# Keeping the S5, GLU and first-norm instructions of a hybrid backbone block in their emitted order on each engine

## Chip, cores and metric

The kernel runs on one core of one Trainium2 chip. The metric is the time of one execution in device microseconds (us). The kernel before takes 1634.49 us, the median of three runs (1630.75, 1634.49 and 1637.27 us).

## What is computed

The block has two layers over 256 latent and 256 context tokens of width 1024. Layer 0 mixes tokens with a bidirectional S5 state-space scan and a GLU, layer 1 with a bidirectional chunked gated DeltaNet; both end in an MLP. Cut to the part that matters here:

```python
h_l = _modulate(_rmsnorm(x, norm1_w[0]), mod_l[0], mod_l[1])      # mod = silu(c) @ ada_w + ada_b, six vectors
a_bar = jnp.exp(lam * dt)
_, h = lax.associative_scan(_linear_recurrence, (a, bu), axis=0)  # both directions, complex
y = jnp.einsum('lbgp,ghp->blgh', h, c_mat).real
y = jax.nn.gelu(y + d_skip * u)
y_a, y_b = jnp.split(y @ w_glu, 2, axis=-1)
x = x + mod_l[2] * (y_a * jax.nn.sigmoid(y_b))                    # GLU, gated residual
h2 = _modulate(_rmsnorm(x, norm2_w[0]), mod_l[3], mod_l[4])       # the first norm behind the GLU
x = x + mod_l[5] * _sqrelu_mlp(h2, mlp_w1[0], mlp_w2[0])
```

Context tokens go through the same weights, with their own modulation. Layer 1 repeats the frame with the DeltaNet mixer.

## The kernel before

**Stages.** The program runs, in order of time: the S5 input (per block of 128 channels b = 0 to 7: coefficient tiles W and V, transposed inputs `sint`, products `xin`), the scan over 63 chunks (`X`, `scanm`, on DVE: 31 steps for one half of the tokens, 32 for the other), the S5 output (`s5_out`: copies `Hs` of the scan state, products `yp`, a gelu `yg`, a transpose back into `yT`), the GLU of the first half of the tokens, GLU(0), then of the second, GLU(1), the norms in front of the MLP (`norm_tile`: a square with its sum, a power for the reciprocal root, transposes `ntp`, scaled copies `hf`, split into `hh` and `hl`), the MLP of layer 0, the DeltaNet layer, and the last MLP.

**Splits.** Float32 products are made of three matmuls. Each operand is split in two, a rounded part (`whi`, `yh`, `hh`) and the rest (`wlo`, `yl`, `hl`). For a GLU weight block of 512 KB (`wraw`, loaded through a ring of four slots) ACT casts `whi`, and POOL and DVE each subtract one half of `wlo` from it; three such pairs are held. A GLU half has 16 blocks: 4 column groups `cg` of 4 blocks, 12 matmuls a block.

**What sets the order.** Five engines (PE matrices, DVE, ACT, POOL vectors, SP the DMA queue) each run their instructions one after another. The work is written as tasks (Python generators), and `drive` (line 316) asks a planner, `Clock`, which step can begin first by its own costs, and so writes out one step after another. This is the emitted order. Every engine call goes through `Engine.__getattr__` (line 254, the call at 268, which is the line of all rows), which gives the instruction a priority that grows with the emitted number. A scheduler behind it then builds each engine's queue: it may let an instruction pass an earlier one that waits. So the order on the chip is near the emitted order, and not equal to it.

**Which part is driven how.** `s5_phase` (line 1240 on) drives three times: S5 input, then scan and `s5_out` of the first half, then `s5_out` of the second half with GLU(0) and the loads and splits of its weights. `tile_backbone` drives GLU(1) with the four norms (line 2148). The main part of the DeltaNet layer is driven with `clock.fill` set (lines 2096 and 2097), its tail with `clock.window = 1.0` (lines 2106 and 2107). The MLPs are written in plain loops, without `drive`.

**The modulation vectors.** `ada00`, `ada01` and `ada02` are three products with 4 MB of weights each (`adaw` tiles of 512 KB that use the same ring of four slots as `wraw`). The scan does not need the last two.

Of the kernel before, what the change touches and what calls it, by code (L numbers as in the profile page):

```python
# [252 lines left out]
class Engine:  # L253
# [3 lines left out]
    def __getattr__(self, op):  # L257
        f = getattr(self.eng, op)
        if not callable(f):
            return f  # L260

        def call(*args, **kw):
            c = self.clock
            p = c.issue(self.name, op, args, kw)
            if c.prio is not None:
                c.tc.cur_priority = c.base + c.prio * 20000 + c.n
                c.n += 1
            r = f(*args, **kw)  # L268
            if c.window is not None and self.name == "tensor" and c.prio is not None:
                c.follow(p[0], r.ins)  # L270
            return r
        return call
# [1944 lines left out]
```

## Time and profile before

| | us |
|---|---|
| median of three runs | 1634.49 |
| the profiled execution, whole | 1630.61 |
| its span, first to last instruction | 1628.8 |
| PE busy in the span | 1467.9 (90%) |
| DVE busy | 1105.0 (68%) |
| ACT busy | 777.4 (48%) |
| POOL busy | 654.3 (40%) |

The granted PE clock is 0.951 on average. The profile gives each instruction a start and an end, and for an idle engine the instruction that released it. PE's share is high because both MLPs and much of the DeltaNet layer are matrix work; in the first 372 us it is lower, and there each stage has another limit. What a change in a stage is worth has to be read from that stage, in a table of busy times by stretch, and then in the rows of the engine that the others wait for.

### The profile page before, as it was taken

To read this page: it belongs to the slowest core of one execution; us is meant where nothing else is said; L and a number is where in the kernel's file an instruction comes from. 1 tells how busy PE (TensorE), PEld (TensorE's weight loads), DVE (VectorE), ACT (ScalarE), POOL (GpSimd) and SP (SyncE) were. 2 spreads that over 40 slices of the span, in tenths; PEclk is the share of its full clock that TensorE was granted. 3 is DMA by queue.
4 is the path that set the end of the run, shared out by engine and by line. 5 is a ranking of instruction groups with operands and counts; after the bars stand their busy time and mean duration, and the time that the engine had idled before them with its cause. 6 is when DMAs were issued, how large, how long until landed. Compare 5 with 4: busy or idle time off the path is not lost.

```text
span 1628.8 us, 31232 instructions
## 1 busy us (share of the span) xinstructions
PE 1467.9 (90%) x12370; PEld 1115.7 (68%) x12370; DVE 1105.0 (68%) x2011; ACT 777.4 (48%) x1637; POOL 654.3 (40%) x510
## 2 busy tenths in 40 slices
PE   6895678989999999997968898989999999989998
PEld 2454456767777777786756676767766665689997
DVE  6977798763343343347998878687869765667666
ACT  3352646543222232216456655656565755554443
POOL 3977033622333233334766543343615400014432
PEclk7997889999999999998989999999998999989999
DMA  9786623463544545331222211111211111536552
GB/s 279 264 290 91 137 98 118 156 211 113 172 147 170 188 158 181 139 106 65 79 77 67 66 54 47 53 47 50 70 39 59 44 57 61 188 127 196 182 192 91
DMA packets 76771, 200.77 MB, mean 123 GB/s; under 512 B 8784, under 2 KB 29008, under 8 KB 76368
## 3 DMA queue, kind: packets, MB, share of 16 engines
q1 hardware_dynamic: 76112, 197.78, 37.1%
q10 hardware_dynamic: 512, 0.98, 0.4%
q8 instruction: 97, 1.59, 0.4%
q14 instruction: 50, 0.41, 0.1%
HBM read 192.71 MB, written 6.03 MB: 122 GB/s over the span
## 4 chain that ended last, share of the span: by engine, by line
PE 62%; DVE 20%; ACT 6%; issue 5%; POOL 4%; DMA 3%; SPq 0%; POOLq 0%; DVEq 0%; ACTq 0%
PE w L268 32%; PE proj L268 8%; PE c L268 6%; DVE cacc L268 3%; PE ada L268 3%; DVE X L268 3%; PE wo L268 2%; POOL wlo L268 2%; DVE wlo L268 1%; DVE U L268 1%; DVE scanm L268 1%; DVE gt L268 1%; PE op L268 1%; PE qs L268 1%; DMA wraw<-in_w_dram 1%
## 5 line engine op out<-in xcount | busy, mean ns | idle before, releaser
L268 ACT CAST whi<-wraw 128x1024 fp32r<-128x1024 f32 x221 | 225.6, 1045 | 259.7 <-PE w L268 140.0
L268 POOL TENSOR_TENSOR wlo<-wraw,whi 128x512 fp32r<-128x512 f32 x129 | 181.7, 1427 | 258.4 <-ACT whi L268 233.6
L268 DVE TENSOR_TENSOR wlo<-wraw,whi 128x1024 fp32r<-128x1024 f32 (+1 forms) x189 | 222.0, 1202 | 79.9 <-ACT whi L268 79.3
L268 PE MATMUL w<-hh,whi 128*128 128x256 f32 (+1 forms) x512 | 170.5, 336 | 0.0
L268 PE MATMUL w<-hl,whi 128*128 128x256 f32 (+1 forms) x512 | 168.9, 331 | 0.0
L268 PE MATMUL w<-hh,wlo 128*128 128x256 f32 (+1 forms) x512 | 168.5, 331 | 0.0
L268 POOL TENSOR_TENSOR sq<-rl 128x512 f32<-128x512 f32 (+1 forms) x64 | 62.5, 977 | 217.1 <-ACT rl L268 213.3
L268 PE MATMUL w<-whi,h1h 128*128 128x512 f32 x384 | 148.8, 395 | 0.0
L268 PE MATMUL w<-whi,h1l 128*128 128x512 f32 x384 | 148.5, 390 | 0.0
L268 PE MATMUL w<-wlo,h1h 128*128 128x512 f32 x384 | 148.4, 389 | 0.0
L268 PE MATMUL proj<-hh,whi 128*128 128x256 f32 (+1 forms) x360 | 130.6, 363 | 10.3 <-ACT pp L268 8.4
L268 DVE TENSOR_TENSOR ma<-w,g 128x512 f32<-128x512 f32 x96 | 65.3, 687 | 103.5 <-PE w L268 103.4
L268 PE MATMUL proj<-hh,wlo 128*128 128x256 f32 (+1 forms) x360 | 125.5, 349 | 1.7 <-POOL wlo L268 1.7
L268 PE MATMUL proj<-hl,whi 128*128 128x256 f32 (+1 forms) x360 | 126.9, 352 | 0.0
L268 DVE SCALAR_TENSOR_TENSOR cacc<-pp,cw,cacc 128x520 f32<-128x520 f32 (+1 forms) x128 | 115.3, 903 | 11.5 <-ACT cacc L268 9.9
L268 POOL TENSOR_TENSOR xr<-xr,ma 128x512 f32<-128x512 f32 x56 | 81.3, 1455 | 95.9 <-DVE ma L268 95.9
L268 PEld LDWEIGHTS w<-hh,whi 128*128 128x128 f32 x512 | 98.0, 192 | 18.1 <-DVE wlo L268 4.2
L268 DVE TENSOR_TENSOR h1l<-sq,h1h 128x512 fp32r<-128x512 f32 (+1 forms) x64 | 35.5, 555 | 106.4 <-POOL sq L268 104.0
L268 PEld LDWEIGHTS w<-hl,whi 128*128 128x128 f32 x512 | 98.2, 192 | 10.5 <-issue 1.9
L268 PEld LDWEIGHTS w<-hh,wlo 128*128 128x128 f32 x512 | 97.9, 192 | 9.8 <-issue 0.8
L268 ACT ACTIVATE v<-c,vsc 64x128 f32<-64x128 f32 x224 | 80.6, 362 | 50.0 <-PE c L268 42.6
L268 POOL TENSOR_TENSOR rstd<-ms,mhalf 128x1 f32<-128x1 f32 (+2 forms) x22 | 17.3, 788 | 191.1 <-DVE ms L268 191.1
(312 smaller groups left out, 3532.2 us busy)
## 6 DMA issues: line engine op xcount, KB each, us to landing
wraw<-in_w_dram SPq DMA_DIRECT2D x128, 512.0 KB, 4.3
adaw<-in_ada_w_dram SPq DMA_DIRECT2D x92, 512.0 KB, 4.8
wraw<-in_w_in_dram SPq DMA_DIRECT2D x48, 512.0 KB, 3.2
wraw<-in_w_glu_dram SPq DMA_DIRECT2D x32, 512.0 KB, 3.3
wraw<-in_w_out_dram SPq DMA_DIRECT2D x16, 512.0 KB, 3.2
Kt<-kd SPq DMA_DIRECT2D x32, 128.0 KB, 4.9
X<-grd SPq DMA_DIRECT2D x32, 128.0 KB, 3.0
V<-in_ada_w_dram SPq DMA_DIRECT2D x4, 512.0 KB, 5.9
```

Of the source, the lines that this page charges most:

```text
L268: r = f(*args, **kw)
```

## The change

Two lines in the helper through which all engine calls go. An instruction of a driven step that is neither in the `fill` part nor has a `window` is tied to the one emitted before it on its engine. The tie is a rule for the scheduler, no semaphore: the engine waits for nothing new, but the queue can no longer be rearranged there.

```diff
             r = f(*args, **kw)
+            if c.prio is not None and not c.fill and c.window is None:
+                c.tc.keep_in_program_order(r)
             if c.window is not None and self.name == "tensor" and c.prio is not None:
                 c.follow(p[0], r.ins)
```

So the tie holds in the three drives of `s5_phase` and in the drive of GLU(1) and the norms. By its condition it does not hold in the main part of the DeltaNet layer (`fill`), nor in that layer's tail (`window` is 1.0 there). No instruction is added or taken away: PE has 13113 in both, DVE 2013, ACT 1555, POOL 515, SP 481. The queues of the MLP of layer 0 are the same in both; in the DeltaNet layer, which is not tied, about 1350 of PE's instructions stand at another place than before, because the scheduler comes to them in another state.

ACT while the first half's output is made. Before (`Hs` of block 5 reads `X0`, `yp_2207` is block 4):

```order
L268 COPY Hs_2202<-X0_83 64x2x128 x4
L268 ACTIVATE yg_2182<-yp_2164 128x256
L268 COPY Hs_2244<-X0_83 64x2x128 x4
L268 COPY mcol0_97<-adat02_2319 128x8x2 x2
L268 ACTIVATE yg_2225<-yp_2207 128x256
L268 COPY Hs_2286<-X0_83 64x2x128 x4
L268 ACTIVATE yg_2271<-yp_2253 128x256
```

The same place with the change:

```order
L268 ACTIVATE yg_2225<-yp_2207 128x256
L268 COPY Hs_2244<-X0_83 64x2x128 x4
L268 COPY arow_2249<-ada02_1930 128x512
L268 ACTIVATE yg_2271<-yp_2253 128x256
L268 COPY Hs_2286<-X0_83 64x2x128 x4
L268 ACTIVATE yg_2309<-yp_2291 128x256
L268 COPY mcol0_97<-adat02_2319 128x8x2 x2
L268 COPY Hs_2335<-X0_83 64x2x128 x4
L268 ACTIVATE yg_2362<-yp_2344 128x256
L268 CAST yh_2393<-yT_1357 128x8x32 x8
```

Before, the copies of the next block stand ahead of a block's gelu (`Hs_2286`, block 6, before `yg_2271`, block 5). Now each block's gelu stands right behind its own copies, and all eight `yh` casts stand behind the last gelu. On DVE the 32 scan steps of the second half now stand entirely ahead of GLU(0)'s subtractions, with only the eight transposes between them; before, `wlo`, `yl` and gate steps of GLU(0) stood among them. `ada02`, which PE did before the scan, now stands between the `yp` of the first half, and its loads behind those of `Kt`.

ACT in the middle of GLU(0), with the change (`whi` are weight blocks, `Hs` reads the second half's state `X1`, `gth` is the gate's tanh):

```order
L268 CAST whi_2574<-wraw_2466 128x1024
L268 CAST yh_2393<-yT_1357 128x8x32
L268 COPY Hs_2583<-X1_84 64x2x128 x2
L268 ACTIVATE gth_2588<-glu_2440 128x256
L268 ACTIVATE gth_2594<-glu_2441 128x256
L268 ACTIVATE yg_2625<-yT_1357 128x256
L268 CAST whi_2634<-wraw_2473 128x1024
L268 CAST whi_2654<-wraw_2513 128x1024
L268 CAST yh_2393<-yT_1357 128x8x32
L268 COPY Hs_2663<-X1_84 64x2x128 x2
L268 ACTIVATE yg_2691<-yT_1357 128x256
L268 CAST whi_2700<-wraw_2559 128x1024
```

Two weight blocks now alternate with one output block, and `Hs` of an output block stands behind the cast of a weight block that needs a freed pair. Before, all `Hs` and `yg` came late, in a bunch, with weight casts done ahead of them. PE has the same pattern: six matmuls of a block, one `yp`, the block's other six, then twelve of the next block.

PE where GLU(1) begins, with the change (`gb` makes the gate's rows, `ntp` the transposes of the norms of tiles 0 and 1):

```order
L268 MATMUL gb_3053<-g1r_3050,consts_63 128x512
L268 MATMUL gb_3056<-g1r_3050,consts_63 128x512
L268 MATMUL ntp_3069<-consts_63,xn_3061 128x128 x4
L268 MATMUL ntp_3081<-consts_63,xn_3061 128x128 x4
L268 MATMUL glu_3093<-whi_2946,yh_2393 128x512
L268 MATMUL glu_3093<-wlo_2947,yh_2393 128x512
L268 MATMUL glu_3093<-whi_2946,yl_2394 128x512
L268 MATMUL glu_3094<-whi_2946,yh_2393 128x512
L268 MATMUL glu_3094<-wlo_2947,yh_2393 128x512
L268 MATMUL glu_3094<-whi_2946,yl_2394 128x512
L268 MATMUL ntp_3109<-consts_63,xn_3101 128x128 x4
L268 MATMUL ntp_3121<-consts_63,xn_3101 128x128 x4
```

Before, 22 matmuls of GLU(1) stood ahead of `ntp_3069` and 28 more ahead of `ntp_3109`. Now none and six do.

## Rows read from the trace of the kernel before

**Rows 1.** Busy times by stretch: us, busy PE, PEld, DVE, ACT, POOL, clock, DMA share.

```profile
179.40:210.10 30.70, 21.20 (x350) 13.70 (x350) 19.82 (x74) 29.92 (x55) 0.00 (x0) 0.91 0.38 129
210.10:233.40 23.30, 14.24 (x49) 10.81 (x49) 22.50 (x59) 6.54 (x9) 8.56 (x6) 0.76 0.25 86
233.40:288.40 55.00, 49.54 (x404) 35.97 (x403) 46.34 (x88) 32.63 (x52) 22.97 (x19) 0.95 0.38 129
288.40:340.40 52.00, 48.74 (x222) 39.10 (x221) 39.57 (x49) 27.13 (x40) 30.15 (x26) 1.00 0.49 173
...
372.00:730.00 358.00, 358.00 (x1668) 276.24 (x1667) 138.24 (x158) 100.21 (x134) 119.95 (x89) 1.00 0.44 152
730.00:1440.00 710.00, 636.76 (x6576) 472.98 (x6574) 552.65 (x1120) 417.38 (x1047) 285.30 (x233) 0.95 0.20 68
```

**Rows 2.** PE's timeline in the first half's output: start, us, instruction [idle, releaser].

```profile
181.35 2.36 PE L268 MATMUL yl<-Kt,U 128*32 128x128 f32 x40 [6.92 <-ACT Hs L268]
...
202.93 1.07 PE L268 MATMUL yp<-V,Hs 128*32 128x128 f32 x28 [0.24 <-ACT Hs L268]
```

**Rows 3.** ACT's timeline there and at the head of GLU(0).

```profile
186.69 0.38 ACT L268 ACTIVATE yg<-yp 128x256 f32<-128x256 f32 x1
...
200.31 2.57 ACT L268 COPY Hs<-X 64x256 f32<-64x256 f32 x4
202.90 0.38 ACT L268 ACTIVATE yg<-yp 128x256 f32<-128x256 f32 x1
...
206.70 2.49 ACT L268 CAST yh<-yT 128x256 fp32r<-128x256 f32 x5
...
221.40 1.05 ACT L268 CAST whi<-wraw 128x1024 fp32r<-128x1024 f32 x1 [1.26 <-PE glu L268]
```

**Rows 4.** PE's timeline in GLU(0), first blocks.

```profile
210.10 0.49 PE L268 MATMUL glu<-whi,yh 128*128 128x512 f32 x1 [2.04 <-ACT whi L268]
...
222.51 0.39 PE L268 MATMUL glu<-whi,yh 128*128 128x512 f32 x1
231.10 0.80 PE L268 MATMUL glu<-wlo,yh 128*128 128x512 f32 x1 [8.20 <-DVE wlo L268]
```

**Rows 5.** DVE's timeline, the end of the second half's scan.

```profile
244.59 0.60 DVE L268 TENSOR_TENSOR X<-X,scanm 128x128 f32<-128x128 f32 x2
```

**Rows 6.** DVE's and POOL's timelines around one split of a weight block.

```profile
264.82 0.69 DVE L268 TENSOR_TENSOR wlo<-wraw,whi 128x512 fp32r<-128x512 f32 x1 [0.16 <-ACT whi L268]
265.43 1.72 DVE L268 TENSOR_TENSOR yl<-yT,yh 128x256 fp32r<-128x256 f32 x1
...
267.50 0.84 DVE L268 COPY Hs<-X 64x256 f32<-64x256 f32 x2
...
264.87 1.78 POOL L268 TENSOR_TENSOR wlo<-wraw,whi 128x512 fp32r<-128x512 f32 x1 [5.36 <-ACT whi L268]
```

**Rows 7.** PE's timeline, the last matmuls of GLU(0) and of GLU(1).

```profile
285.97 0.39 PE L268 MATMUL glu<-whi,yl 128*128 128x512 f32 x1
286.29 1.12 PE L268 MATMUL gb<-g1r,consts 32*128 32x512 f32 x2
...
340.04 0.39 PE L268 MATMUL glu<-whi,yl 128*128 128x512 f32 x1
```

**Rows 8.** Timelines of ACT and PE, the first norm beside GLU(1).

```profile
290.21 1.07 ACT L268 ACTIVATE xn<-xr 128x1024 f32<-128x1024 f32 x1 [2.45 <-DVE xr L268]
...
294.09 1.03 PE L268 MATMUL ntp<-consts,xn 128*128 128x128 f32 x8
...
297.76 0.46 ACT L268 ACTIVATE hf<-ntp,mcol,modc 128x128 f32<-128x128 f32 x1 [3.19 <-DVE hf L268]
...
299.90 0.62 ACT L268 CAST hh<-hf 128x512 fp32r<-128x512 f32 x1
```

**Rows 9.** DMA issues of the page: instruction, count, KB each, us to landing.

```profile
adaw<-in_ada_w_dram SPq DMA_DIRECT2D x92, 512.0 KB, 4.8
...
wraw<-in_w_glu_dram SPq DMA_DIRECT2D x32, 512.0 KB, 3.3
```

## The prediction

> **What bounds the kernel now.** I read the table of busy times by stretch first, because an average over the span says nothing here. The MLP of layer 0 is all PE (358 us busy in 358), and the DeltaNet layer nearly so [rows 1]. Both stand behind the part that is tied. So time won or lost by 372 us is won or lost at the end, and the reader should look at the stages before it. From 179.4 to 210.1 ACT is busy 29.92 of 30.70 us: the first half's output is bound by ACT. From 210.1 to 233.4 DVE is busy 22.50 of 23.30 us while PE has 14.24. From 233.4 on PE is the busy one, with 49.54 of 55.00 and 48.74 of 52.00 us [rows 1].
>
> Then the timelines. The first half's output does not wait for the scan. PE idles 6.92 us and then does `yl` at 181.35, whose operand `Kt` comes from DMA [rows 2]. At the head of GLU(0) PE starts at 210.10, and stands still for 8.20 us until 231.10, since DVE's half of a `wlo` is late [rows 4]. DVE is late because it still works on the second half's scan, which ends at 245.20 [rows 5]. GLU(0)'s last matmul ends at 286.36 and GLU(1)'s at 340.43 [rows 7]. These two ends are what I follow.
>
> **S5 input and first half of the scan: no term.** All of `ada01` but its last weights now stands on PE ahead of the first `sint`. `ada02` leaves the stage. The first makes the inputs start later, the second takes waits for weights out of their middle. I take the two as equal. A gain would not arrive in any case: behind the scan the output waits for `yl` [rows 2], and the chain of strips and DMAs that feeds it keeps its order. A loss would have to exceed that slack.
>
> **First half's output: -2.6 and +1.2 a block.** Before, the copies of the next block fill ACT while PE makes a block's `yp`, so a block costs copies and gelu, 2.57 + 0.38 = 2.95 us [rows 3]. Now ACT does copies, waits for PE, does the gelu, and only then copies again. From the end of the copies at 202.88 to the end of `yp` at 204.00 are 1.12 us [rows 2, 3]. A block costs 2.57 + 1.12 + 0.38 + 0.1 for signals = 4.2 us. The first gelu ended at 187.07 [rows 3], with one set of copies ahead of it that now comes later: 184.5. Seven more blocks end at 184.5 + 29.4 = 213.9. The `ada02` loads between them: two tiles a block, and a tile lands 4.8 us after its issue with four slots in flight [rows 9], so a pair lies inside 4.2 us each; I take 0, and 1.2 a block for five blocks if each pair waits a full landing and PE (6 us) as the bad end.
>
> **Head of GLU(0): +11.4.** Now the eight `yh` casts and the first `whi` come behind the last gelu, 8 x 0.5 + 1.05 = 5.0 us on ACT [rows 3]. DVE has two gate scalings, eight `yl` and one `wlo` behind the last transpose. At 0.69 each, the nearest row of its kind, this is 7.6 us [rows 6]. PE starts at 213.9 + 7.6 = 221.5, against 210.10 [rows 4].
>
> **Rest of GLU(0).** A matmul costs 48.74 / 222 = 0.22 us, I take 0.23 [rows 1], a block of twelve 2.8. The first four blocks are nearly ready when PE starts: 4 x 2.8, two `yp` of 1.12, one wait of 3 = 16.4 us, to 237.9. Before, the same four blocks end about 233.4, so half of the late start is won back: the scan no longer stands in DVE's way.
>
> The other twelve blocks go in six pairs with an output block in each. Take the moment at which PE ends a block and frees a `whi` as 0. ACT casts until 1.05. DVE subtracts its half, 0.69, to 1.8. POOL's half, beside it, takes 1.78 and ends at 2.9. `yl` of the output block is next on DVE and took 1.72, until 0.5 after POOL's end (267.15 against 266.65) [rows 6], so 3.4. `Hs` on DVE 0.84 [rows 6], 4.25. `yp` ends 1.12 later, at 5.4. PE has done six matmuls by 1.4 and waits 2.9 us. Six and twelve matmuls at 0.23 follow: 9.5 us a pair, where the work alone is 6.6. Six pairs are 57. Three ends of a column group add gate steps on DVE ahead of the `yp` addition. I count 0.8 for each, about one step of 0.69. GLU(0) ends at 237.9 + 57 + 2.4 = 297.3, against 286.36: +10.9.
>
> That DVE's `yl` stands still for POOL's half is what the rows show. The Trainium skill ("SBUF — State Buffer", section "Who interferes with whom") says that the two share a port pair as an exclusive lock, so that the second to issue blocks until the first is done. By it POOL's half would begin only after DVE's 0.69 and end 0.2 us later, and six pairs would cost 1 us more. The rows show an overlap of 0.6, and I keep their sum.
>
> **GLU(1): +6.** The gate's row `g1r` is loaded behind a weight block that itself waits for GLU(0)'s last splits: about 0.3, one landing of 3.3 us [rows 9] and 1.1 for the second transfer, 4.7 us after GLU(0). `gb` takes 1.12 [rows 7]. From the norm's square to the end of its `ntp` 4.9 us passed (290.21 to 295.12) [rows 8]; the square, 1.07, fits into the wait, 3.8 are left. So PE's first six matmuls begin at 9.6 and end at 11.0. The second norm on ACT is behind four `hf` and two `hh` of the first, 4 x 0.46 + 2 x 0.62 = 3.1 us from 9.6 [rows 8]. Then 4.9, six matmuls: 19.0. Fifteen blocks of 2.76 are 41.4: GLU(1) takes 60.4 us, against 54.07 before [rows 7]. Before, both norms lay beside matmuls that did not need them, and that cover is gone. The last matmul ends at 357.7, against 340.43: **+17.3**.
>
> **After it: no term.** Norms of tiles 2 and 3 and the head of the MLP keep their waits; the loads they need are not tied. The DeltaNet layer's queue is rearranged without being tied. PE idles there 710 - 636.76 = 73 us [rows 1]. I count 0, and a tenth of it, 7 us, on either side.
>
> **The sum.** 1630.61 + 17 = 1647.6 us, against the profiled execution. That one lies 3.9 us below the median of the three runs. I say **1647**. Over 0.5% from the median of before, about 8 us, is what a measurement can tell from no change.
>
> **Rivals.**
> *The waits are half as long (same, 25%).* If POOL's half does not hold DVE, `yl` ends at 2.5 and a pair takes 8.5: 6 us less. If the gate's row is there in time, another 5.9 less. 1647.6 - 11.9 = 1636. For it: with the order freed, PE ran 49.54 of 55.00 us in this stretch [rows 1], so the durations allow it. Against: the 1.72 of `yl` [rows 6].
>
> *The scan is gone from DVE, and this decides (faster, 20%).* Now the second half's scan is done before GLU(0). The 8.20 us wait [rows 4] and the slow start of the second half's output, which could not begin before 245.20 [rows 5], are both gone. If a pair waits less than 1 us, GLU(0) costs 16 x 2.8 + 8 x 1.12 = 53.8 us from 221.5, ends at 275.3, 11.1 earlier than before, and GLU(1) as before leaves 1619.5. It turns on the wait per pair: at 0.9 us the end is as before, and I have 2.9. Against it: cast, split and copies behind a freed slot are 1.05 + 0.69 + 0.84 = 2.6 alone [rows 3, 6], and PE covers 1.4.
>
> *The loads starve the output (slower, inside the 55%).* The 6 us from above: 1653.
>
> *The tie does little.* In the tail it does not hold, by its condition. If only the DeltaNet layer's rearrangement is felt, the result is 1631 give or take 7; this lies in the two cases above.
>
> **How the numbers follow.** My sum and the starved case have 55% (slower), the half-waits case 25% (same), the gone scan 20% (faster). The range goes from 1622, below the half-waits case by 14 for the DeltaNet layer on top of smaller waits, to 1660, the sum with 6 us of starved loads and 7 of the DeltaNet layer. Inside it, the forecast's own range is 1640 to 1660.
>
> **What would show it.** ACT idles about 1.2 us in each block of the first half's output. The scan's last step ends near 215, not 245. GLU(0) begins near 221 and ends near 297, with a wait of about 3 us ahead of six `yp`. PE waits twice, 9.6 and 6.6 us, at the head of GLU(1). GLU(1) ends near 358. It is wrong if GLU(0) ends before 286 (the scan decides), if GLU(1)'s head has no wait, or if the two ends agree but the DeltaNet layer differs by over 7 us.

## The result and the profile after

| | us |
|---|---|
| before, median of 4 runs | 1632.74 (1630.75 to 1637.27) |
| after, median of 4 runs | 1715.41 (1714.2 to 1717.05) |
| ratio | 1.0485, 95% interval 1.0449 to 1.0521 |
| span of the profiled execution, after | 1713.5 (before 1628.8) |
| mean granted PE clock, after | 0.927 (before 0.951) |

The kernel became slower, as forecast, but by 79 to 83 us and not by 17. First the places, from the timelines of both kernels:

| us from the span's start | before | after | change | forecast |
|---|---|---|---|---|
| first transpose `sint` of S5's input | 58.0 | 84.1 | +26.1 | |
| scan's first addition | 130.9 | 166.0 | +35.1 | 0 |
| scan ends | 245.2 | 253.6 | +8.4 | -30 |
| GLU(0), first matmul | 210.1 | 259.8 | +49.7 | +11.4 |
| GLU(0), last matmul | 286.4 | 354.4 | +68.0 | +10.9 |
| GLU(1), last matmul | 340.4 | 423.3 | +82.9 | +17.3 |
| end of the span | 1628.8 | 1713.5 | +84.7 | +17 |

So the whole loss is there at 423 us, and the MLP and the DeltaNet layer add 1.8. Busy times of the kernel after by stretch, in the columns of [rows 1], for S5's input, the output with the head, GLU(0), GLU(1), the MLP and the DeltaNet layer. The second, third and fourth stretch are cut where these stages now lie; the others are the stretches of the kernel before (S5's input now lasts until 166 us):

```profile
57.50:130.90 73.40, 43.85 (x325) 28.69 (x325) 38.10 (x46) 17.13 (x40) 57.77 (x32) 0.73 0.35 119
210.10:259.81 49.71, 30.86 (x394) 15.74 (x394) 28.83 (x116) 31.68 (x56) 1.50 (x2) 0.85 0.71 236
259.81:354.36 94.55, 73.17 (x450) 53.12 (x448) 47.12 (x79) 32.74 (x51) 33.08 (x23) 0.79 0.28 95
354.36:423.31 68.95, 54.80 (x235) 44.15 (x236) 36.56 (x53) 30.80 (x45) 33.49 (x27) 0.85 0.41 140
372.00:730.00 358.00, 348.35 (x1657) 266.84 (x1658) 145.87 (x175) 115.38 (x160) 123.90 (x95) 0.98 0.47 161
730.00:1440.00 710.00, 645.39 (x6554) 490.80 (x6552) 534.62 (x1044) 396.37 (x983) 309.92 (x249) 0.95 0.20 66
```

The same view of the kernel before, for S5's input, GLU(0) and GLU(1):

```profile
57.50:130.90 73.40, 70.44 (x1075) 45.79 (x1074) 55.19 (x81) 39.19 (x94) 62.86 (x30) 0.98 0.69 234
210.10:286.36 76.26, 62.25 (x449) 46.27 (x449) 67.35 (x144) 37.85 (x59) 31.05 (x24) 0.89 0.34 116
286.36:340.43 54.07, 50.32 (x224) 39.64 (x225) 41.09 (x52) 28.49 (x42) 30.63 (x27) 1.00 0.49 171
```

S5's input is the surprise. PE was busy 70.44 of 73.40 us and is busy 43.85 now, DVE 55.19 and now 38.10, ACT 39.19 and now 17.13. That three engines fall together suggests that they wait for each other in a ring. PE's timeline of the kernel after shows where (start, us, instruction, count [idle before, releaser]):

```profile
59.41 3.64 PE L268 MATMUL ada<-adaw,crep 128*32 128x512 f32 x16
65.17 1.05 PE L268 MATMUL ada<-adaw,crep 128*32 128x512 f32 x4 [2.12 <-DMA adaw<-in_ada_w_dram]
...
69.61 1.05 PE L268 MATMUL ada<-adaw,crep 128*32 128x512 f32 x4 [2.12 <-DMA adaw<-in_ada_w_dram]
70.86 3.88 PE L268 MATMUL ada<-adaw,crep 128*32 128x512 f32 x12 [0.21 <-DMA adaw<-in_ada_w_dram]
...
84.12 1.04 PE L268 MATMUL sint<-consts,W 128*128 128x128 f32 x8
88.00 1.97 PE L268 MATMUL ebx<-eb,sel 128*128 128x64 f32 x8 [2.83 <-DVE W L268]
...
101.54 1.97 PE L268 MATMUL ebx<-eb,sel 128*128 128x64 f32 x8 [6.47 <-DVE W L268]
115.59 1.97 PE L268 MATMUL ebx<-eb,sel 128*128 128x64 f32 x8 [6.05 <-DVE W L268]
130.47 1.97 PE L268 MATMUL ebx<-eb,sel 128*128 128x64 f32 x8 [6.12 <-DVE W L268]
```

Two things stand in PE's queue. From 59.41 to 83 us it makes the products of the conditioning row `ada01` at the pace of their weights, with `sint` behind them, which before began at 58.0. After that, each expansion `ebx` waits for DVE to finish a `W`. The expansions have two banks, so the one for block b+2 can only start when block b has been used. In the emitted order it stands ahead of transposes that are ready, and those transposes would free the `W` buffers that DVE needs. From 57.5 to 130.9 us DVE waits 26.9 us for `sint`, in three waits.

GLU(0) shows a second ring. One pair of blocks in the timelines of PE, ACT, DVE and POOL of the kernel after:

```profile
303.36 0.63 PE L268 MATMUL glu<-whi,yh 128*128 128x512 f32 x1
303.79 0.63 PE L268 MATMUL glu<-wlo,yh 128*128 128x512 f32 x1
...
306.72 0.40 PE L268 MATMUL glu<-whi,yh 128*128 128x512 f32 x1
306.96 0.39 PE L268 MATMUL glu<-wlo,yh 128*128 128x512 f32 x1
...
311.06 0.41 PE L268 MATMUL yp<-V,Hs 128*32 128x128 f32 x4 [1.43 <-ACT Hs L268]
312.57 1.58 PE L268 MATMUL yp<-V,Hs 128*32 128x128 f32 x28 [1.09 <-DVE Hs L268]
...
308.35 1.05 ACT L268 CAST whi<-wraw 128x1024 fp32r<-128x1024 f32 x1 [2.38 <-PE glu L268]
309.31 0.66 ACT L268 CAST yh<-yT 128x256 fp32r<-128x256 f32 x1
309.76 1.25 ACT L268 COPY Hs<-X 64x256 f32<-64x256 f32 x2
...
309.43 0.69 DVE L268 TENSOR_TENSOR wlo<-wraw,whi 128x512 fp32r<-128x512 f32 x1 [2.39 <-ACT whi L268]
310.04 1.69 DVE L268 TENSOR_TENSOR yl<-yT,yh 128x256 fp32r<-128x256 f32 x1
311.75 0.76 DVE L268 COPY Hs<-X 64x256 f32<-64x256 f32 x2
...
309.48 1.77 POOL L268 TENSOR_TENSOR wlo<-wraw,whi 128x512 fp32r<-128x512 f32 x1 [1.63 <-ACT whi L268]
```

ACT casts the next `whi` only when PE has freed a buffer, and both halves of `Hs` stand behind: ACT's behind the cast, DVE's behind `wlo` and `yl`. PE stands still for 1.43 and 1.09 us ahead of `yp` in this pair, and for much the same in the other six. Behind six of the seven pauses the granted clock falls to 0.50, the level of 1.2 GHz: matmuls start 0.43 us apart (303.36, 303.79), and only later, at 2.4 GHz, 0.24 (306.72, 306.96). Behind the pauses around 290 us it stays at 1.00. In the whole of GLU(0) the granted clock is 0.79, before 0.89.

The head of GLU(1), PE's timeline of the kernel after:

```profile
360.61 2.15 PE L268 MATMUL gb<-g1r,consts 32*128 32x512 f32 x4 [6.26 <-DMA g1r<-arow]
365.63 1.97 PE L268 MATMUL ntp<-consts,xn 128*128 128x128 f32 x8 [2.87 <-DVE xn L268]
...
374.02 1.94 PE L268 MATMUL ntp<-consts,xn 128*128 128x128 f32 x8 [3.87 <-DVE xn L268]
```

### The profile page after: what moved, and what is told of

It reads as the page before. It is cut to its first block, busy times and chain, and to the rows that moved or that the text cites. A ratio compares the mean times of both kernels' runs of the same rounds, so it can differ in the third digit from the quotient of the medians.

```text
span 1713.5 us, 31246 instructions
## 1 busy us (share of the span) xinstructions
PE 1487.5 (87%) x12370; PEld 1135.7 (66%) x12370; DVE 1083.0 (63%) x2011; ACT 780.4 (46%) x1637; POOL 660.8 (39%) x510
## 3 DMA queue, kind: packets, MB, share of 16 engines
q1 hardware_dynamic: 76112, 197.78, 35.1%
## 4 chain that ended last, share of the span: by engine, by line
PE 64%; DVE 18%; DMA 6%; ACT 6%; issue 4%; POOL 1%; SPq 1%; ACTq 0%; POOLq 0%; DVEq 0%
PE w L268 30%; PE proj L268 8%; PE c L268 6%; PE glu L268 4%; DVE cacc L268 3%; PE wo L268 3%; PE ada L268 2%; DVE W L268 2%; DMA adaw<-in_ada_w_dram 1%; PE yp L268 1%; PE qs L268 1%; DVE gt L268 1%; ACT whi L268 1%; DVE wlo L268 1%; DVE vc L268 1%
## 5 line engine op out<-in xcount | busy, mean ns | idle before, releaser
L268 POOL TENSOR_TENSOR wlo<-wraw,whi 128x512 fp32r<-128x512 f32 x129 | 187.0, 1465 | 314.4 <-ACT whi L268 291.3
L268 DVE TENSOR_TENSOR wlo<-wraw,whi 128x1024 fp32r<-128x1024 f32 (+1 forms) x189 | 216.7, 1174 | 119.7 <-ACT whi L268 116.9
L268 PE MATMUL proj<-hl,whi 128*128 128x256 f32 (+1 forms) x360 | 129.4, 359 | 0.0
L268 DVE SCALAR_TENSOR_TENSOR cacc<-pp,cw,cacc 128x520 f32<-128x520 f32 (+1 forms) x128 | 116.1, 909 | 12.9 <-ACT cacc L268 11.1
L268 ACT ACTIVATE v<-c,vsc 64x128 f32<-64x128 f32 x224 | 80.7, 362 | 59.7 <-PE c L268 42.3
L268 POOL TENSOR_TENSOR rstd<-ms,mhalf 128x1 f32<-128x1 f32 (+2 forms) x22 | 17.3, 788 | 193.6 <-DVE ms L268 176.9
```

## The experiments

All runs alter the condition of the tie alone. `drive` counts its calls in `c.nd`: 1 is S5's input, 2 the scan with the first half's output, 3 the second half's output with GLU(0), 4 GLU(1) with the norms. A cost is the ratio less one, times the 1636 to 1639 us of the kernel before on the same chip. Beside it stands the end of GLU(1) in the one profiled execution against 340.4, as a second measure that leaves out what comes later: the part behind GLU(1) takes 1287 to 1301 us in these executions, with no pattern that I could tie to what was held, and the runs of the kernel before reach from 1629 to 1644 us.

### One stretch at a time

```diff
-            if c.prio is not None and not c.fill and c.window is None:
+            if c.prio is not None and not c.fill and c.window is None and c.nd == 1:
```

and 2, 3, 4 in place of 1 in the next three.

> The tie holds only in the first planned stretch (S5's input). Theory A, each stretch pays where it is tied: the scan's first addition starts near 166 us instead of 130.9, and the 35 us reach the end, about 1668 us (1655 to 1680). Theory B, the stretches cost together because one that stays free fills its own idle time with what came late: the scan starts late all the same, but the free stretches behind it take back a third or more, 1645 to 1655 us.

> The tie holds only in the second planned stretch (the scan and the output of its first half). Theory A: the first half's output is paced by the held order (4.2 us a block) and costs a few us, while the scan's second half ends up to 17 us sooner because VectorE gives it all of its time; 1633 us (1627 to 1640). Theory B: with its inputs on time the held scan feeds the free GLU sooner, 1620 to 1627 us.

> The tie holds only in the third planned stretch (output of the second half and GLU(0)). Theory A: the head (7 us) and GLU(0) that is 25 us longer remain, about 1665 us (1655 to 1675), first to last matmul of GLU(0) near 101 us. Theory B: with its inputs on time the held order waits less, 1640 to 1650 us, GLU(0) at 85 us or less.

> The tie holds only in the last planned stretch (GLU(1) and the first norm). Both theories: 8 us, 1641 us (1637 to 1646). Theory A has the four single costs add up to 75 to 83 us; theory B has them add up to 50 us or less.

| held | median us | ratio, 95% interval | cost us | GLU(1) ends later by |
|---|---|---|---|---|
| S5 input | 1677.44 | 1.0254 (1.0211 to 1.0296) | 41.6 | 43.0 |
| scan | 1632.74 | 0.9978 (0.9958 to 0.9999) | -3.6 | -3.1 |
| GLU(0) | 1675.72 | 1.0255 (1.0209 to 1.0301) | 41.7 | 41.9 |
| GLU(1) | 1655.79 | 1.0123 (1.0079 to 1.0167) | 20.1 | 14.0 |

S5's input pays its own price: the first addition is at 165.1, and nothing behind it takes that back (GLU(0) 76.0 us long, 76.3 before). The scan costs nothing; it ends at 236.1, 9 us sooner, but it also begins 8 us sooner (123.0 against 130.9), so it is hardly shorter. GLU(0) begins 9 us later and is 9.4 us shorter. GLU(0) and GLU(1) alone cost more than expected. The four add up to 99.8 us, or 95.8 at GLU(1)'s end, where the whole change has 79 and 82.9: neither theory said that. Part of the excess is a long wait that only the run with GLU(0) alone has. The free scan is still running there, and PE waits for `yl` once for 10.0 us (its waits in GLU(0)):

```profile
PE yp L268 <- ACT Hs L268: 12.1, 8, 2.1
PE glu L268 <- DVE yl L268: 10.0, 1, 10.0
```

In the changed kernel this wait is 1.6 us, since S5's delay lets the held scan finish first.

### S5's input, taken apart

```diff
+ ... and c.nd == 1 and self.name == "tensor"                          # s5_input_pe_alone
+ ... and c.nd == 1 and c.prio != 9                                    # s5_input_row_free
+ ... and c.nd == 1 and self.name == "tensor" and c.prio != 9          # s5_input_pe_row_free
+ ... and c.nd == 1 and self.name != "tensor"                          # s5_input_all_but_pe
+ ... and c.nd == 1 and self.name == "tensor" and c.prio not in (2, 9) # s5_input_pe_expansion_free
```

Rank 9 is the task of the conditioning rows `ada01` and `ada02`; on PE, rank 2 is `ebx` and one small product of the modulation. Where a rank is left free, the tie goes to the last instruction that is itself tied.

> The tie holds only in S5's input, and there only on TensorE. Theory A, TensorE's order is the cost (the 16 weight products of the next conditioning row stand ahead of the first transposes of W and wait for their weights): first transpose near 84 us as in the changed kernel, first addition of the scan near 150, 1668 to 1680 us. Theory B, the cost comes from the order of the transfers or of several engines together: TensorE alone in order costs under 15 us, first addition of the scan before 131 us, 1637 to 1650 us.

> The tie holds in S5's input on all engines, except for the task of the next conditioning rows (its products on TensorE, its copies, its transfers of bias and row), which is left free. Theory A, about 26 of the 37 us are these products ahead of the transposes: first transpose at 58 to 62 us, the scan's first addition at 122 to 132 us, 1640 to 1655 us. Rival, the products only fill time in which TensorE would wait for W on VectorE anyway: first transpose early, but the scan's first addition still after 140 us and the time over 1665 us.

> The tie holds in S5's input on TensorE alone, with the task of the conditioning rows left free. What is left of the cost is then the order of the expansions, transposes and input products among themselves. Theory A, they wait in a ring for VectorE's W and each other: 18 to 26 us as with all engines held, 1655 to 1664 us, the scan's first addition at 132 to 140 us. Theory B, that rest came from the other engines' order: under 8 us, 1637 to 1646 us, first addition before 124 us.

> The tie holds in S5's input on VectorE, ScalarE, GpSimd and SyncE, and TensorE is free. Theory A, TensorE's order makes all of the 40 us: under 8 us, 1637 to 1646 us, the scan's first addition before 124 us. Theory B, the other engines' order closes the same ring by itself: 15 us or more, over 1653 us.

> The tie holds in S5's input on TensorE alone, with the conditioning rows and the expansions ebx left free (with them the one product of the modulation, which is in the same rank). Theory A, the expansions are the rest of the cost: there are two banks for them, the one for block b+2 waits until VectorE has made W of block b, and in TensorE's held order transposes and input products that are ready stand behind it; free, the 26 us fall to under 10, 1637 to 1648 us, the scan's first addition before 126 us. Theory B, the order of transposes and input products is enough by itself: 18 us or more remain, over 1656 us.

| held in S5's input | ratio, 95% interval | cost us | first `sint` | scan's first addition |
|---|---|---|---|---|
| PE alone | 1.0247 (1.0209 to 1.0286) | 40.5 | 82.1 | 159.4 |
| all, rows free | 1.0161 (1.0126 to 1.0197) | 26.4 | 60.2 | 150.2 |
| PE alone, rows free | 1.0161 (1.0135 to 1.0186) | 26.4 | 59.7 | 151.9 |
| all but PE | 1.0055 (1.0035 to 1.0075) | 9.0 | 58.4 | 144.8 |
| PE alone, rows and `ebx` free | 0.9968 (0.9949 to 0.9987) | -5.2 | 57.4 | 129.4 |

PE's order alone costs as much as that of all engines, 40.5 and 41.6 us. The order of the others isn't free: without PE's it costs 9.0 us, a little over the 8 of theory A, the first addition is 14 us late, and GLU(1) ends 15.1 us later. With the rows freed the first transpose is back at 60, as expected, but only 14 of the 40 us go: the expectation of 26 was a miss. With the expansions freed as well, nothing is left. So 14 and 26 are the shares in this order of freeing. The expansions were never freed alone, and that the late `sint` and the ring of the expansions overlap is a likely reason for the miss, not a shown one. The expectations from `s5_input_row_free` on seem to count the scan's start from its first product `scanm`, which comes at 115.6 us in the kernel before and 154.1 in the one after; by that count the five runs have 153.7, 136.4, 144.7, 129.1 and 120.8. DVE's waits in the two last PE runs, with PE's rows free (57.5 to 145 us):

```profile
DVE W L268 <- PE sint L268: 19.3, 3, 8.8
DVE W L268 <- ACT X L268: 10.3, 1, 10.3
```

and with the expansions free too:

```profile
DVE wtmp L268 <- PE sint L268: 2.5, 1, 2.5
```

The small product of rank 2 was freed with `ebx` and wasn't tried by itself. PE makes it at 53.1 us in the last run and at 57.4 in the one before, so up to 4 of the 26 us may be its.

### GLU(0), taken apart

```diff
+ ... and c.nd == 3 and self.name == "tensor"               # glu0_pe_alone
+ ... and c.nd == 3 and self.name == "vector"               # glu0_vector_alone
+ ... and c.nd == 3 and self.name in ("tensor", "vector")   # glu0_pe_and_vector
+ ... and c.nd == 3 and self.name != "vector"               # glu0_all_but_vector
+ ... and c.nd == 3 and self.name != "tensor"               # glu0_all_but_pe
+ ... and c.nd == 3 and self.name != "scalar"               # glu0_scalar_free
```

> The tie holds in the third stretch (GLU(0)) on TensorE alone. Theory A: with ScalarE and VectorE free to bring the state copies sooner, TensorE's order costs 5 to 15 us, 1640 to 1652 us. Theory B: all of the cost of this stretch is here, 1670 to 1680 us.

> The tie holds in the third stretch (GLU(0)) on all engines but ScalarE. Theory A, ScalarE's order is the cost: each copy of the scan's state stands behind the gelu of the block before and reaches TensorE late; its 12 us of waits and the chain behind them go, GLU(0) from 108 to about 90 us, 1650 to 1660 us. Theory B, TensorE's order alone decides (output products emitted ahead of products that are ready): no gain, 1670 to 1680 us.

> The tie holds in the third stretch (GLU(0)) on VectorE alone. Theory A: on VectorE the remainders of the next weights, which wait for a free buffer of split weights and so for TensorE, stand ahead of the copy of the scan's state; VectorE's queue alone closes that ring: 25 to 40 us, 1663 to 1678 us, GLU(0) over 95 us. Theory B, it takes both queues: under 10 us, 1638 to 1648 us.

> The tie holds in the third stretch (GLU(0)) on all engines but VectorE. Theory A: ScalarE's queue, in which the casts of the next weights stand ahead of its half of the state copies, closes the same ring too: 20 to 38 us, 1658 to 1676 us. Theory B, only VectorE's queue does: under 10 us, 1638 to 1648 us.

> The tie holds in the third stretch (GLU(0)) on TensorE and VectorE alone. Theory A, the cost is the ring of the two: TensorE waits at the output products for VectorE's state copies, VectorE ahead of them for split weights whose buffers TensorE has yet to free; 30 to 40 us as with all but ScalarE held, 1668 to 1680 us. Theory B, the costs only add (TensorE alone 0, VectorE alone 16): 12 to 22 us, 1650 to 1661 us, and the rest was GpSimd's or SyncE's order.

> The tie holds in the third stretch (GLU(0)) on all engines but TensorE. Theory A, without TensorE's order the ring is open, since products that are ready run while the state copies are late: 10 to 22 us, 1648 to 1661 us. Theory B, VectorE's and ScalarE's queues close it by themselves: 30 us or more, over 1668 us.

| held in GLU(0) | ratio, 95% interval | cost us | GLU(0) us | GLU(1) ends later by |
|---|---|---|---|---|
| PE | 0.9997 (0.9977 to 1.0016) | 0 | 81.5 | 10.3 |
| DVE | 1.0099 (1.0076 to 1.0122) | 16 | 87.0 | 19.7 |
| all but DVE | 1.0093 (1.0068 to 1.0119) | 15 | 85.3 | 11.7 |
| all but PE | 1.0170 (1.0142 to 1.0198) | 28 | 93.5 | 25.9 |
| PE and DVE | 1.0178 (1.0151 to 1.0205) | 29 | 111.8 | 41.1 |
| all but ACT | 1.0218 (1.0166 to 1.0270) | 36 | 111.0 | 40.2 |
| all | 1.0255 (1.0209 to 1.0301) | 42 | 108.4 | 41.9 |

No single queue is the cause, and several of these expectations missed. PE's order, which alone cost 40 us in S5's input, is free here by the time, as long as the others may bring the state copies early; the profiled execution, the longest of ten, does end GLU(1) 10.3 us later. DVE alone costs 16 to 20. PE and DVE together delay GLU(1)'s end by 41 us, as much as all engines, though only 29 of it show in the time; freeing ACT changes nothing that clears the noise (36 against 42 us, intervals that overlap). With PE and DVE held, PE's waits in the pairs are at their full size, all on DVE's `Hs` (beside them stands one wait of 8.5 us for ACT's, and one of 8.5 for `yl`):

```profile
PE yp L268 <- DVE Hs L268: 18.5, 7, 2.9
```

With all but PE held, PE stands at `yp` only once, for 2.5 us; it waits once for `yl`, and for the split weights instead:

```profile
PE glu L268 <- DVE yl L268: 9.2, 1, 9.2
PE glu L268 <- ACT whi L268: 6.2, 9, 1.5
PE glu L268 <- POOL wlo L268: 5.2, 6, 1.1
```

So the wait at `yp` in each pair needs PE's and DVE's order together. By the time alone the two don't stand out: with one of them free the others' order still costs 15 to 28 us, and the two together cost 29. Why 41 us at GLU(1)'s end are 29 in the time with these two held, and 42 with all, stays open; it lies behind GLU(1).

### GLU(1)

```diff
+ ... and c.nd == 4 and self.name == "tensor"
```

> The tie holds in the last stretch (GLU(1) and the first norm) on TensorE alone. Theory A, TensorE's order is the cost there (the norm's transposes stand ahead of GLU products that are ready and wait 11 us for the normed rows): 10 to 20 us, 1648 to 1660 us. Theory B, it needs the other engines' order too: under 6 us, 1634 to 1644 us.

Measured: 1642.0 us, ratio 1.0025 (1.0005 to 1.0044), 4 us. Theory B: it needs the other engines' order too. PE's wait for the normed rows with all engines held, 287 to 355 us:

```profile
PE ntp L268 <- DVE xn L268: 10.8, 2, 6.2
```

and with PE alone held, 288 to 346 us:

```profile
PE ntp L268 <- DVE xn L268: 4.7, 1, 4.7
```

Freed, DVE and ACT bring the second norm in time for PE's unchanged order. Of the 20 us with all held, 12.7 lie in GLU(1) (66.8 us against 54.1), and 6 behind it, inside the spread of that part.

### The change with the two tasks left free, and a faster version

```diff
+ ... and (c.nd > 1 or c.prio != 9 and (self.name, c.prio) != ("tensor", 2))                           # hold_all_two_free
+ ... and (c.nd == 1 and self.name == "tensor" and c.prio not in (2, 9) or c.nd == 2)                  # hold_pe_and_scan
```

> The changed kernel's tie in all four stretches, with two things left free in S5's input: the task of the conditioning rows, and on TensorE the expansions ebx. Theory A, these two are the S5 input's share of the loss also where everything else is held: the scan's first addition returns from 154 to 115 to 130 us, and of the 82.7 us some 30 to 40 go, 1675 to 1687 us. Rival, the late stretches are held by something else and the gain is lost behind the scan: 1700 us or more.

> The two parts that alone stood at or just under the kernel before, together: S5's input held on TensorE without rows and expansions (ratio 0.9968 alone), and the scan's stretch held whole (0.9978 alone). If both are gains and add up: ratio 0.992 to 0.997, about 9 us under the kernel before. Rival, neither is a gain of the order (GLU(0) and the recurrence behind take them back): ratio 0.998 to 1.004.

With everything held as in the change but for these two tasks, the time is 1680.3 us, ratio 1.0272 (1.0244 to 1.0300): 35 us of the loss are gone. The first addition is at 136.6 in place of 166.0, and the first `scanm`, whose 154 us the expectation starts from, at 124.9. GLU(0) begins at 230.4 in place of 259.8. Theory A holds.

The second kernel takes 1624.68 us, the median of 8 runs, against 1635.75: ratio 0.9936 (0.9909 to 0.9963). That is 0.6% faster than the kernel before, and the first theory holds: the two single ratios multiply to 0.9946. S5's input and GLU(0) of this kernel, in the columns of [rows 1]:

```profile
57.50:124.50 67.00, 56.37 (x920) 42.81 (x922) 54.45 (x80) 37.98 (x93) 65.30 (x31) 0.92 0.38 124
215.00:282.00 67.00, 59.00 (x449) 44.48 (x449) 57.55 (x112) 38.10 (x60) 33.10 (x24) 0.94 0.44 148
```

DMA is busy 0.38 of the first stretch, in the kernel before 0.69 from 57.5 to 130.9 us. Of the 108 products of the conditioning rows (`ada<-adaw`) that the kernel before makes from 57.5 to 130.9 us, 52 are left there, and the scan begins 6 us sooner. GLU(0) then begins 5 us later but takes 67.0 us in place of 76.3, with the scan gone from DVE at 234.4, 11 us sooner. All of this is already there with the scan's stretch alone held:

```profile
57.50:130.90 73.40, 61.80 (x1202) 47.15 (x1202) 62.75 (x85) 39.15 (x95) 68.06 (x32) 0.95 0.43 148
```

There too 52 products are left, the scan begins 8 us sooner and GLU(0) takes 66.8 us. So what these rows explain is the part of the scan's stretch. The tie in S5's input adds to it (3.6 us less with the scan's stretch, 10.5 with both; GLU(1) ends 3.1 and 6.1 us sooner), and what it changes stays open.

## Why the prediction was right in sign and wrong in size

**"S5 input and first half of the scan: no term": this step failed, by 35.1 us.** It saw both movements, `ada01` ahead of the first `sint` and `ada02` out of the stage, and set them equal without pricing either. The trace had what it needed: PE was busy 70.44 of 73.40 us there, so little room was left for waits put into PE's queue. And it didn't look for the expansions at all: 26 of the 40 us remain with the rows freed, and go with the expansions. The 6.92 us of PE's wait at `yl` [rows 2], which it took for a slack that a loss must exceed, were none. The `yl` waits for `Kt`, which is loaded from strips made of S5's own `V` and `W`, so a late S5 input makes the whole chain late. ACT issues the last of the strips (`kd`) at 163.53 us in the kernel before and at 196.99 in the one after:

```profile
163.53 2.60 ACTq L268 DMA_DIRECT2D kd<-strip  x4
196.99 3.23 ACTq L268 DMA_DIRECT2D kd<-strip  x4
```

The waiting `yl` starts at 181.35 and at 216.16, 34.8 us later. (There the profile names the load of `adab`, which was issued right behind the last `Kt` and is used only at 235.6.) The Trainium skill ("PSUM — Partial Sum Buffer", section "Engine vs sequencer instructions") says that the queues of ACT, DVE and POOL are strict first in, first out, and that matmuls start in program order. The trace agrees: the first `sint` starts at 84.1 us, behind the last product of `ada01` at 82.3.

**First half's output: right.** 4.2 us a block were forecast, 29.4 for seven; the gelus end at 221.48 and 252.51, 31.0 for seven. ACT's timeline of the kernel after shows the step as written, copies, a wait of 1.17 us, the gelu, copies; it answers to [rows 3]:

```profile
231.14 2.60 ACT L268 COPY Hs<-X 64x256 f32<-64x256 f32 x4
234.90 0.38 ACT L268 ACTIVATE yg<-yp 128x256 f32<-128x256 f32 x1 [1.17 <-PE yp L268]
235.31 2.58 ACT L268 COPY Hs<-X 64x256 f32<-64x256 f32 x4
```

The 0.1 us for signals in the forecast stands in no row; here the copies follow a gelu after 0.03. The first gelu, less S5's 35.1, ends at 186.4 and not 184.5.

**Head of GLU(0): the number right, the reason half.** 7.6 us were forecast from the last gelu to PE's start, 7.3 passed (252.51 to 259.81). But PE was held by the gate's row `g1r`, issued at 247.4 and used at 257.8, and `yl` came behind the scaling that waited for it. That the number fits is luck.

**Scan ends near 215: right, once moved.** 253.6 less 35.1, and less the 3.2 us by which output and head came later than forecast, is 215.3.

**Rest of GLU(0): 75.8 forecast, 94.55 measured; mis-sized by 18.8.** The ring was described as it runs, and its waits were sized well. PE's waits in GLU(0):

```profile
PE yp L268 <- ACT Hs L268: 10.0, 7, 1.5
PE yp L268 <- DVE Hs L268: 7.9, 7, 1.3
PE glu L268 <- DVE wlo L268: 1.8, 1, 1.8
PE glu L268 <- DVE yl L268: 1.6, 1, 1.6
```

These are 21.3 us, with 2.6 in each of seven pairs; the forecast had 3 at the start, 2.9 in each of six pairs and 2.4 for the gate steps, 22.8 in all. What was wrong is PE's own time, 73.2 us busy where the forecast has 192 x 0.23 + 8 x 1.12 = 53.1. It took 0.23 us for every matmul. Of the 181 steps between matmuls that follow each other directly, 34 are 0.39 to 0.43, ten, right behind a pause or a `yp`, are 0.59, and four are 0.31 to 0.34: 10.7 us more than at 0.23. `yp` was priced at 1.12 and takes 0.41 plus 1.5 to 1.9, only once 0.41 plus 1.07, at full clock: 16.6 us for eight where 9.0 were forecast. The rest, some 2 us, lies in the last matmuls ahead of a `yp` or a wait, whose full length counts. Against the same steps at full clock (0.23, 0.34 behind a `yp`, 1.07 for the 28 of a `yp`), an estimate of the low clock's part is 14 of these 20 us. The forecast of waits was not carried into the clock that follows them.

The collision of `yl` with POOL's `wlo` came as [rows 6] had it: 1.69 us in each pair, against 0.61 to 0.63 where POOL is idle. By the Trainium skill ("SBUF — State Buffer", section "Who interferes with whom") whichever issues first has the pair of ports and the other blocks. The trace agrees: POOL, issued 0.05 behind DVE's half, takes 1.77 in place of 1.27, and `yl` ends 0.48 us after POOL. The 1 us that the prediction worked out from this rule was rightly left out of its sum: the wait is already inside the 1.78 that it took for POOL's half.

**GLU(1): 60.4 forecast, 68.95 measured; 8.6 short.** Both waits at its head are there. The gate's row came 6.25 us after GLU(0), not 4.7: SP issued it 3.5 us after the last matmul, behind loads that waited for buffers, where 0.3 was assumed; from its issue to `gb` were then 2.7 us, where 4.4 were assumed. PE's first six products begin 12.9 us in, not 9.6, and those behind the second norm 21.3 us in, not 17.6. From there to the last matmul are 47.7 us, not 42.8: 21 products `w` of the MLP stand among the last ones, about 2.8 us that the forecast did not count, two waits are 1.2, and the first five steps at the low clock about 1.1. The low clock of this stage (0.85 on average, 1.00 before) lies in its head: over these 47.7 us it is 0.98.

**After it: right.** 1.8 us against 0, give or take 7. Since this part varies by 14 us between the executions here, one pair of them shows no more than that.

The sum of the misses is 35.1 + 3.2 (output and head) + 18.8 + 8.6 = 65.7 us, which with the forecast 17.3 makes the 82.9 measured at GLU(1)'s end, within rounding. Of the rivals, the gone scan was right about the scan and wrong about what decides: in the changed kernel, and in the run with the two tasks free, the scan ends before GLU(0) begins (253.6 and 259.8, 225.5 and 230.4), and GLU(0) still takes 94.6 and 90.0 us. The half-long waits didn't come, nor did the starved output: between its blocks PE waits at most 0.36 us for the loads of `ada02`.

## What to carry to other kernels

Before an order is fixed, ask of each engine's queue, PE's first, what stands behind an instruction that can wait: a product of weights just loaded, or a step two buffers ahead. On an engine that is nearly always busy, as PE was in S5's input, there is little idle time to hide such a wait in, and if the work behind it leads to what it waits for, it is paid once per block, as at the expansions here. Ordering can also help: the tie on the scan's stretch kept the products of `ada02` out of S5's input, the scan began 8 us sooner, and together with the tie on PE's transposes and input products the kernel gained 0.6%.

## What was unexpected of the hardware

A wait on PE cost more than its own length. In GLU(0) PE idles 2.6 us ahead of `yp` in each pair. Behind six of the seven pauses the granted clock falls to 0.50, and the matmuls of 128x512 step by 0.43 us before they come back to 0.23 or 0.24; behind one it stays at 1.00, and why that one differs was not looked into. The slow steps are 10.7 us over 0.23 a matmul, 2.7 of them in the first 12 us, where the clock was already low at the stage's start, in a stage whose waits at `yp` are 17.9.
